# A decoder layer on one Trainium2 core: five edits to the order of background work and to the weight buffers

## The chip, the cores and the metric

The kernel is one launch on one core of a Trainium2 chip. The metric is device time in microseconds (us), the median of repeated runs; less is better. The core has a matmul engine (PE, and PEld for its weight loads), a vector engine (DVE), a scalar engine (ACT), GpSimd (POOL), and SyncE (SP), which issues most of the DMAs.

## The reference

One inference step of one hybrid decoder layer for 512 prompt tokens and 32 sample tokens (8 sequences of 4), model width 2048, all in float32:

```python
xn = rmsnorm(x, g_mix)
q, k, v, iq, ik, iw, xb, yb, qm = split(xn @ w_in)
o_attn = dsa_attend(...)        # indexer scores, top-k keys per query, softmax over those keys
o_lru = rg_lru(conv4(xb)) * gelu(yb)
o_mem = softmax(qm @ mk.T * MEM_SCALE) @ mv
gates = sigmoid(xn @ w_gate)
x = x + sum_n(gates[n] * (o[n] @ w_br[n])) @ w_o
h = rmsnorm(x, g_ffn)
s = (h @ w_peer_q) scored against two sets of 128 sub keys per head, 8 heads; top 16 of the 16 x 16 sums
y = sum over the chosen 16384-row experts of  softmax(s) * gelu(u[e] . h) * v[e]
out = rmsnorm(x + y, g_final)
```

The sample tokens read paged key and value caches, and states of the convolution and of the recurrence.

## The kernel before

**Products.** Every float32 weight chunk of 128 x 1024 (512 KB) is streamed once: SP issues the DMA into a tile `raw` (L242), ACT rounds it to `hi` (L222), DVE forms `lo = raw - hi` (L223), and PE multiplies hi by the high and low part of the activations and lo by the high part, so 24 matmuls of up to 320 columns for one chunk in the last stage. `raw` has a ring of RAW = 3 buffers, `hi` and `lo` of HL = 3 (L173); `widen(stack, raw, hl)` (L230) adds buffers from a pool that lives as long as the stack.

**Order of work.** The 544 tokens are done in two parts: columns 0 to HA - 1 and the rest. The program is written as a foreground of projections with four queues of generators beside it (`bg`, `bg2`, `bg3`, `bg4`, class `Background`, L141). `pump()` runs in the foreground's inner loop, and each queue advances by its `rate` for eight pumps. Each engine executes its instructions in the order in which the program issues them, and so does SP's queue of DMAs. The rates therefore fix the order of the instructions on each engine.

**Stages.** Memory keys and norms to about 300 us; `branches(0)` to about 600; `merge` (L922) of the first part to 1060; `output_proj` to 1150; queries of the first route; `branches(1)`, 1300 to 1792; `merge(HA, ...)` to 2206; `output_proj(HA, ...)` to 2338; the second route's queries, each followed by one `up` (L1310), to 2600; gate matrices with further ups to 2914; then 16 groups of eight `z` (L1432) and `down` (L1447), to 4473, and the last norm. In `branches(1)` the indexer's rounds of maximum and replacement run on DVE (L637, L638), attention heads (L820 scores, L830 transposes of the softmax `ex`, L837 values) sit in `bg2`, memory heads (L485 scores, L491 transposes of `mex`) in `bg`, and eight recurrence channels (`lru`, L736) in `bg4`, each entered after its two projections xb and yb. The experts of the first 96 prompt tokens are gathered row by row beside all this (`bg3`): POOL issues a 1 MB gather (L1189), paced by a matmul, and DVE multiplies it (L1237 for u, L1245 for v), some 2.3 us each, in three `row` buffers.

**The last stage.** `ups` 0 to 49 (AHEAD_UP = 50) are done before it, each stored to DRAM (`ge_dram`, L1317) and read back as `gl` (L1428) when its z is formed; from group 6 on the ups run beside the downs. `zh` and `zl` have ZB = 16 buffers, `gl` has GL = 4, and the stage has no added `raw` buffers. `acc` (2.5 MB) is loaded before group 0's down (L1464).

Of the kernel before, what the change touches and what calls it, by code (L numbers as in the profile page):

```python
# [8 lines left out]
F = mybir.dt.float32  # L9
# [3 lines left out]
AF = mybir.ActivationFunctionType  # L13
OP = mybir.AluOpType
# [9 lines left out]
HA = NS + SEQ // 2  # L24
# [14 lines left out]
NX = NG - 128  # L39
NTA = T - NG  # L40
N1 = HA - NG
GL = 4
ZB = 16
AHEAD_UP = 50

CH_Q, CH_K, CH_V, CH_IQ, CH_IK, CH_XB, CH_YB, CH_QM, NCH = 0, 8, 10, 12, 20, 21, 29, 37, 45
# [130 lines left out]
def program(tc, ins, outs):  # L177
    nc = tc.nc
# [212 lines left out]
    def branches(part):  # L391
# [154 lines left out]

        def mem_channels():
            for h in range(4):
                qm = []
                for i in range(2):  # L550
                    s = staged(CH_QM + 2 * h + i)
                    if first:
                        nc.vector.tensor_copy(qms[:, 2 * h + i], s[:, :P0])
                    qm.append(s)
                bg.add(mem_head(h, qm))
# [177 lines left out]
            nc.sync.dma_start(scv, ins["sconv"])  # L733
            nc.sync.dma_start(slr, ins["slru"])

        def lru(c, xb, yb):  # L736
            def v(i):
                return vec[:, i + c:i + c + 1]

# [52 lines left out]
            if first:  # L792
                nc.gpsimd.tensor_copy(hl[:, c, 1:], bt(hs)[:, :, NT - 1])
            yield
            nc.scalar.activation(ig, yb, AF.Gelu_apprx_tanh)
            nc.vector.tensor_tensor(ig, hs, ig, op=OP.mult)
            nc.sync.dma_start(o_dram[8 + c, :, cols], ig)
            yield
# [96 lines left out]
        if first:  # L895
            bg2.add(*[attn_sample(pr) for pr in range(NB // 2)])
        bg4.rate = 2.2
        bg2.rate = 2.2 if first else 1.1
        if not first:
            memo = ExitStack()  # L900
            open_memory()
            bg.rate = 0.8
            mem_channels()
        for c in range(8):
            xb = staged(CH_XB + c)
            yb = staged(CH_YB + c)
            bg4.add(lru(c, xb, yb))
        bg2.drain()
        bg.drain()
        bg4.drain()  # L910
# [11 lines left out]
    def merge(c0, x, mp_, side):  # L922


        mo = ([], [])
        n_ = x[0].shape[-1]
        os_ = ExitStack()
        op_ = pool(f"lm{c0}", os_, side=side)
        m = [mp_.tile([128, n_], F, name=f"m{e}", tag="ml", bufs=ND + 1) for e in range(ND)]
        for i, n in enumerate((2, 0, 1)):  # L930
            op = ([op_.tile([128, n_], R, name=f"oh{k}") for k in range(8)],
                  [op_.tile([128, n_], R, name=f"ol{k}") for k in range(8)])
            with urgent():
                for k in range(8):
                    raw = op_.tile([128, n_], F, name="oraw", tag="sg", bufs=4)
                    nc.sync.dma_start(raw, o_dram[8 * n + k, :, c0:c0 + n_])
                    split(op[0][k], op[1][k], raw)
            sgs = {}
            for d in range(ND + GLAG):
                if d < ND:  # L940
                    pg = project(ins["w_gate"][n * ND + d], [x], ND, ps_p)
                    sgs[d] = op_.tile([128, n_], F, name="sg", tag="sg", bufs=4)
                    with urgent():
                        nc.scalar.activation(sgs[d], pg, AF.Sigmoid)
                if d < GLAG:
                    continue
                e = d - GLAG
                sg = sgs.pop(e)
                pu = project(ins["w_br"][n, e], [op], 8, ps_p)
                with urgent():  # L950
                    if i == 0:
                        nc.vector.tensor_tensor(m[e], pu, sg, op=OP.mult)
                    else:
                        nc.vector.tensor_tensor(sg, pu, sg, op=OP.mult)
                        nc.gpsimd.tensor_tensor(m[e], m[e], sg, op=OP.add)
                    if i == 2:
                        mo[0].append(mp_.tile([128, n_], R, name=f"mh{e}"))
                        mo[1].append(mp_.tile([128, n_], R, name=f"ml{e}", tag="ml", bufs=ND + 1))
                        split(mo[0][e], mo[1][e], m[e])
        os_.close()  # L960
        return mo

    def output_proj(c0, mo, xg, o0, rs):

        n_ = rs.shape[-1]
        wo = ExitStack()
        wp = pool(f"wp{c0}", wo)
        ssum = wp.tile([128, n_], F, name="ssum")
        for d in range(ND):
            xr = wp.tile([128, n_], F, name="xr", bufs=2)  # L970
            nc.sync.dma_start(xr, ins["xT"][d, :, c0:c0 + n_])
# [4 lines left out]
            nc.sync.dma_start(x2_dram[d, :, c0:c0 + n_], x2)  # L976
            scaled_split(xg[0][:, d, o0:o0 + n_], xg[1][:, d, o0:o0 + n_], x2, V_GFFN + d)
            add_square(ssum, x2, wp.tile([128, n_], F, name="sq"), d == 0, nc.vector if d >= 12 else nc.gpsimd)
        inv_rms(rs, ssum, n_, ps_w, "w1")
        wo.close()  # L980


    branches(0)
# [9 lines left out]
    xgfs = ExitStack()  # L993
    xgfp = pool("xgf", xgfs, side="right")
    xgF = [xgfp.tile([128, ND, HA], R, name=f"xgF{i}") for i in range(2)]
    output_proj(0, mF, xgF, 0, rs[:, :HA])
    mfs.close()

    gs_ = ExitStack()
# [294 lines left out]
    for d in range(ND):  # L1294
        x2 = map_.tile([128, N1], F, name="x2r", bufs=2)
        nc.sync.dma_start(x2, x2_dram[d, :, NG:HA])
        scaled_split(xgd[0][:, d, :N1], xgd[1][:, d, :N1], x2, V_GFFN + d)
    output_proj(HA, mA, xgd, N1, rs[:, HA:])
    wide.close()
    mas.close()  # L1300
    rps = ExitStack()
# [79 lines left out]
                yield  # L1381
            nc.sync.dma_start(g_dram[g0 + i], gs)

    for t, (c0, rows) in enumerate(tiles):
        token_rms(3 + t, HA + c0, rows)
    xg2 = [x[:, :, N1:] for x in xgd]
    bg.rate = 1.2
    bg3.rate = 0.3
    share["pool"] = 0
    pairs(route2, lambda c: query(c, xg2, HA), up)  # L1390
    ups = iter(range(16, AHEAD_UP))
    while bg.queue:
        up(next(ups))
# [10 lines left out]
    bg2.rate = 2.8  # L1404
    bg3.rate = 0.85
    for j in ups:
        up(j)
    bg2.drain()
    ras.close()
    rts.close()  # L1410
# [5 lines left out]
    zp = pool("zp", zs0)  # L1416
    acc = zp.tile([128, ND, NTA], F, name="acc")
    zt = {}

    def gated(j):  # L1420
        if j % 4 == 0:
# [35 lines left out]
    for g in range(16):  # L1457
        bg3.rate = 0.52 if 8 * g < AHEAD_UP else 0.72
        for j in range(8 * g + 2 if g else 0, min(8 * g + 10, 128)):
            if j >= AHEAD_UP:  # L1460
                up(j)
            gated(j)
        if g == 0:
            nc.sync.dma_start(acc, x2_dram[:, :, NG:].rearrange("k p t -> p k t"))  # L1464
        down(g)
    inv_rms(ssum, ssum, NTA, ps_w, "w1")
# [53 lines left out]
```

## Time and profile before

| | us |
|---|---|
| median of 3 runs | 4498.55 (4497.03 to 4500.84) |
| the profiled execution | 4492.66 |
| its span in the trace | 4490.9 |
| PE busy | 4179.3 (93%) |
| DVE busy | 3440.3 (77%) |
| ACT busy | 1931.0 (43%) |
| POOL busy | 1164.4 (26%) |
| DMA moved | 1232.82 MB, 275 GB/s over the span |

Busy time is a mean over stages. An engine that waits is shown with the releaser that ended the wait, in the form [idle <-releaser]. A row of the timeline gives start and length in us, engine, line, operation and tiles; SPq rows are DMA issues. PEclk and the granted clock are shares of full speed, and 0.5 is the lower of the two levels (1.2 of 2.4 GHz).

### The profile page before, as it was taken

The page shows a single profiled execution, that of the slowest core. Times are in us where ns is not written, and L with a number is a line of the kernel's source. Part 1 is how long each engine was busy: PE and PEld are TensorE (multiplying, and loading weights), DVE is VectorE, ACT ScalarE, POOL GpSimd, SP SyncE. Part 2 cuts the span into 40 slices and gives each one's busy share as a digit, 9 for nine tenths or more (in the row PEclk, how much of TensorE's full clock was granted, in tenths as well). Part 3 has the DMA queues.
Part 4 walks back from the last instruction along what each step waited for, and adds up shares of the span by engine and source line. Part 5 has one row for each costly group of instructions (what it writes and reads, how often), then busy time and mean ns, then how long its engine had stood idle before and what let it go on. Part 6 is the DMA issues. An engine that isn't in the chain of part 4 may idle for free. (4 is left out here: it accounts for less than half of the span.)

```text
span 4490.9 us, 75736 instructions
## 1 busy us (share of the span) xinstructions
PE 4179.3 (93%) x29283; PEld 3985.9 (89%) x29283; DVE 3440.3 (77%) x5235; ACT 1931.0 (43%) x2942; POOL 1164.4 (26%) x1295
## 2 busy tenths in 40 slices
PE   8999899999989776999889899989999999999998
PEld 7869699999977765999889899989999999999897
DVE  6547444455788876898888899979877899887887
ACT  5434653344433348444443368633333333333333
POOL 3022410001244233244333331212122222222223
PEclk9999999999999988999999999989999999999999
DMA  7656555556545766999996679999969999997995
GB/s 261 227 191 219 156 161 176 165 175 196 177 141 181 264 231 218 354 385 370 345 330 234 235 272 360 372 355 357 329 230 348 357 360 361 359 345 270 351 367 194
DMA packets 383562, 1232.82 MB, mean 275 GB/s; under 512 B 51552, under 2 KB 169056, under 8 KB 322272
## 3 DMA queue, kind: packets, MB, share of 16 engines
q1 hardware_dynamic: 314592, 747.69, 49.2%
q0 software_dynamic: 68608, 480.28, 27.9%
q8 instruction: 230, 3.77, 0.3%
q14 instruction: 132, 1.08, 0.1%
HBM read 1167.50 MB, written 60.22 MB: 273 GB/s over the span
## 5 line engine op out<-in xcount | busy, mean ns | idle before, releaser
L222 ACT CAST hi<-raw 128x1024 fp32r<-128x1024 f32 x1140 | 1191.6, 1049 | 1661.2 <-PE mm L272 661.0
L223 DVE TENSOR_TENSOR lo<-raw,hi 128x1024 fp32r<-128x1024 f32 x1140 | 1425.6, 1254 | 532.7 <-ACT hi L222 526.0
L272 PE MATMUL mm<-xgd,hi 128*128 128x320 f32 (+1 forms) x4608 | 1025.2, 311 | 8.0 <-ACT hi L222 8.0
L272 PEld LDWEIGHTS mm<-xgd,hi 128*128 128x128 f32 x4608 | 776.0, 191 | 9.7 <-ACT hi L222 9.5
L272 PE MATMUL mm<-xgd,lo 128*128 128x320 f32 (+1 forms) x2304 | 720.3, 313 | 28.8 <-DVE lo L223 28.5
L1447 PE MATMUL mm<-zh,hi 128*128 128x320 f32 x2048 | 636.0, 311 | 39.3 <-ACT zh L222 24.3
L1447 PE MATMUL mm<-zh,lo 128*128 128x320 f32 x2048 | 638.9, 312 | 9.7 <-DVE lo L223 9.6
L1447 PE MATMUL mm<-zl,hi 128*128 128x320 f32 x2048 | 634.9, 310 | 0.0
L272 PE MATMUL mm<-xF,hi 128*128 128x288 f32 x2976 | 618.2, 301 | 0.6 <-DVE xF L223 0.6
L272 PE MATMUL mm<-xA,hi 128*128 128x256 f32 x2976 | 556.9, 288 | 19.7 <-ACT hi L222 19.6
L1189 POOL DMA_INDIRECT row<-in_un,idx x224 | 323.5, 1444 | 934.5 <-PE mm L272 224.3
L1245 DVE SCALAR_TENSOR_TENSOR gacc<-row,hv,gacc 128x2048 f32<-128x2048 f32 x221 | 523.0, 2367 | 28.6 <-DMA row<-in_vn,idx 14.1
L1189 POOL DMA_INDIRECT row<-in_vn,idx x224 | 325.4, 1453 | 844.4 <-PE mm L272 209.3
L1237 DVE SCALAR_TENSOR_TENSOR row<-row,xnat 128x2048 f32<-128x2048 f32 x224 | 515.1, 2299 | 21.7 <-DMA row<-in_un,idx 12.3
L272 PEld LDWEIGHTS mm<-xA,hi 128*128 128x128 f32 x2976 | 469.4, 193 | 47.8 <-issue 25.8
L272 PEld LDWEIGHTS mm<-xF,hi 128*128 128x128 f32 x2976 | 481.9, 188 | 22.3 <-issue 18.8
L272 PEld LDWEIGHTS mm<-xgd,lo 128*128 128x128 f32 x2304 | 439.9, 191 | 39.7 <-DVE lo L223 39.1
L272 PE MATMUL mm<-xF,lo 128*128 128x288 f32 x1488 | 445.7, 300 | 0.0
L272 PE MATMUL mm<-xA,lo 128*128 128x256 f32 x1488 | 429.4, 289 | 12.8 <-DVE lo L223 12.6
L1447 PEld LDWEIGHTS mm<-zh,hi 128*128 128x128 f32 x2048 | 386.8, 189 | 41.9 <-ACT zh L222 24.8
L1447 PEld LDWEIGHTS mm<-zh,lo 128*128 128x128 f32 x2048 | 386.7, 189 | 18.5 <-DVE lo L223 18.1
L1447 PEld LDWEIGHTS mm<-zl,hi 128*128 128x128 f32 x2048 | 386.7, 189 | 0.6 <-DVE zl L223 0.5
(374 smaller groups left out, 6349.8 us busy)
## 6 DMA issues: line engine op xcount, KB each, us to landing
raw<-in_u SPq DMA_DIRECT2D x256, 512.0 KB, 7.1
raw<-in_v SPq DMA_DIRECT2D x256, 512.0 KB, 6.8
raw<-in_w_gate SPq DMA_DIRECT2D x192, 512.0 KB, 5.2
raw<-in_w_in SPq DMA_DIRECT2D x180, 512.0 KB, 4.6
raw<-in_w_br SPq DMA_DIRECT2D x96, 512.0 KB, 4.1
raw<-in_w_o SPq DMA_DIRECT2D x64, 512.0 KB, 4.8
raw<-in_w_pq SPq DMA_DIRECT2D x64, 512.0 KB, 4.2
g_dram<-gs SPq DMA_DIRECT2D x10, 2048.0 KB, 10.4
```

The source lines that it names most:

```text
L222: nc.scalar.copy(hi, src)
L223: eng.tensor_tensor(lo, src, hi.bitcast(F), op=OP.subtract)
L272: last["mm"] = nc.tensor.matmul(p[:, i, :n], a[:, s], chunk(b[which], u + k), start=(u + k == 0 and pr == 0), stop=(u + k == k_chunks - 1 ...
L1189: i = nc.gpsimd.indirect_dma_start(out=r, out_offset=None, in_=ins[table], in_offset=bass.IndirectOffsetOnAxis(ap=ind[:, s:s + 1], axis=0))
L1237: j = nc.vector.scalar_tensor_tensor(r, r, 1.0, xn, op0=OP.mult, op1=OP.mult, accum_out=h)
L1245: j = nc.vector.scalar_tensor_tensor(acc, r, h, acc, op0=OP.mult, op1=OP.add)
L1447: last["mm"] = nc.tensor.matmul(p[:, 0, :NTA], a[:, s], b, start=(k == 0 and pr == 0), stop=(k == 7 and pr == 2))
```

## The change

1. In `branches(1)` the attention queue `bg2` stands still (rate 0.0 in place of 1.1) until memory head 2 is entered, then runs at 1.15; `bg` runs at 1.0 in place of 0.8. In both parts each `lru` is entered after its first projection xb, and waits with its gelu until yb is there.
2. In the last branch of the second `merge`, the adds of e >= 8 go to DVE in place of POOL.
3. `output_proj` returns its `inv_rms` as a closure; in the second part this runs after the projection of query 0 (with `ssum` in a longer-lived pool), and `token_rms` after query 2.
4. The last three of the 50 early ups are issued after the first ten z, ahead of group 0's down.
5. The last stage gets two more `raw` buffers (`widen(zs0, 2, 0)`); ZB falls from 16 to 13 and GL from 4 to 3.

```diff
-GL = 4
-ZB = 16
+GL = 3
+ZB = 13
...
         def mem_channels():
             for h in range(4):
+                if h == 2 and not first:
+                    bg2.rate = 1.15
...
-        def lru(c, xb, yb):
+        def lru(c, xb, late):
...
-            nc.scalar.activation(ig, yb, AF.Gelu_apprx_tanh)
+            while not late:
+                yield
+            nc.scalar.activation(ig, late[0], AF.Gelu_apprx_tanh)
...
-        bg2.rate = 2.2 if first else 1.1
+        bg2.rate = 2.2 if first else 0.0
...
-            bg.rate = 0.8
+            bg.rate = 1.0
...
-            xb = staged(CH_XB + c)
-            yb = staged(CH_YB + c)
-            bg4.add(lru(c, xb, yb))
+            late = []
+            bg4.add(lru(c, staged(CH_XB + c), late))
+            late.append(staged(CH_YB + c))
...
-                        nc.gpsimd.tensor_tensor(m[e], m[e], sg, op=OP.add)
+                        adds = nc.vector if c0 and i == 2 and e >= 8 else nc.gpsimd
+                        adds.tensor_tensor(m[e], m[e], sg, op=OP.add)
...
-        ssum = wp.tile([128, n_], F, name="ssum")
+        ssum = (sums or wp).tile([128, n_], F, name="ssum")
...
-        inv_rms(rs, ssum, n_, ps_w, "w1")
         wo.close()
+        return lambda: inv_rms(rs, ssum, n_, ps_w, "w1")
...
-    output_proj(HA, mA, xgd, N1, rs[:, HA:])
+    finish = output_proj(HA, mA, xgd, N1, rs[:, HA:], xgp)
...
-    for t, (c0, rows) in enumerate(tiles):
-        token_rms(3 + t, HA + c0, rows)
...
-    pairs(route2, lambda c: query(c, xg2, HA), up)
+
+    def between(c):
+        if c == 0:
+            finish()
+        if c == 2:
+            for t, (c0, rows) in enumerate(tiles):
+                token_rms(3 + t, HA + c0, rows)
+        up(c)
+
+    pairs(route2, lambda c: query(c, xg2, HA), between)
...
     for j in ups:
-        up(j)
+        if j < AHEAD_UP - 3:
+            up(j)
...
+    widen(zs0, 2, 0)
...
         if g == 0:
+            for j in range(AHEAD_UP - 3, AHEAD_UP):
+                up(j)
             nc.sync.dma_start(acc, x2_dram[:, :, NG:].rearrange("k p t -> p k t"))
```

**Place 1: PE in the second part, where attention head 0 waits for the last rounds of selection.** Before (mm is a projection, ex the attention's softmax, kT the keys):

```order
L272 MATMUL mm_16981<-xA1_87,hi_17035 128x256
L272 MATMUL mm_16981<-xA0_86,lo_17036 128x256
L830 MATMUL w1_16221<-cst_75,ex_16189 128x128 x3
L820 MATMUL w1_16260<-kT_91,qh_16178 128x512
L830 MATMUL w1_16301<-cst_75,ex_16266 128x128 x4
L837 MATMUL w1_16328<-pT_16182,vN_92 128x256 x3
```

Now, the first attention scores on PE in this part (they carry L824; mex is the memory heads' softmax):

```order
L272 MATMUL mm_17187<-xA0_86,lo_17232 128x256
L491 MATMUL w1_16387<-cst_75,mex_16382 128x128 x2
L497 MATMUL w1_16428<-mpT_16330,mv_16327 128x256 x2
L497 MATMUL w1_16464<-mpT_16330,mv_16327 128x256 x2
L824 MATMUL w1_16500<-kT_91,qh_16495 128x384
L485 MATMUL w1_16528<-mk_16523,stage_16300 128x256
L485 MATMUL w1_16528<-mk_16523,stage_16402 128x256
L491 MATMUL w1_16539<-cst_75,mex_16534 128x128 x2
L834 MATMUL w1_16558<-cst_75,ex_16506 128x128 x3
```

Memory head 0 now stands where attention head 0 stood: its scores (L485) come at place 9199 of PE's order, its transposes (L491) at 9519 and 9618, and the attention's first scores at 9621; before, these were at 9095 and its first transposes at 9517.

**Place 2: PE behind the last projection of the second part.** Before:

```order
L272 MATMUL mm_18774<-xA0_86,lo_18778 128x256
L764 MATMUL w1_18282<-xc_18263,w_rg_18280 128x256
L764 MATMUL w1_18303<-xc_18263,w_ig_18301 128x256
L764 MATMUL w1_18449<-xc_18430,w_rg_18447 128x256
L764 MATMUL w1_18470<-xc_18430,w_ig_18468 128x256
L764 MATMUL w1_18599<-xc_18592,w_rg_18597 128x256
L764 MATMUL w1_18605<-xc_18592,w_ig_18603 128x256
```

Now (L766 is the recurrence's gate product, L764 before):

```order
L272 MATMUL mm_18774<-xA0_86,lo_18778 128x256
L834 MATMUL w1_17990<-cst_75,ex_17946 128x128 x3
L824 MATMUL w1_18047<-kT_91,qh_17706 128x512
L834 MATMUL w1_18082<-cst_75,ex_18053 128x128 x4
L841 MATMUL w1_18115<-pT_17939,vN_92 128x256 x3
L841 MATMUL w1_18115<-pT_17939,vN_92 128x128
L824 MATMUL w1_18166<-kT_91,qh_17937 128x384
L766 MATMUL w1_18182<-xc_18151,w_rg_18180 128x256
L766 MATMUL w1_18203<-xc_18151,w_ig_18201 128x256
L834 MATMUL w1_18216<-cst_75,ex_18172 128x128 x3
L824 MATMUL w1_18271<-kT_91,qh_17937 128x512
L834 MATMUL w1_18312<-cst_75,ex_18277 128x128 x4
```

Behind the last projection three recurrence channels remain, as before, and now one and a half attention heads as well.

**Place 3: SP's queue at the start of the last stage.** Before:

```order
L242 DMA raw_31895<-in_v 128x1024
L1423 DMA gt_31648<-g_dram_85 128x10x128
L1317 DMA ge_dram_82<-ge_31637 128x320
L1428 DMA gl_31652<-ge_dram_82 128x320
L1428 DMA gl_31659<-ge_dram_82 128x320
L1428 DMA gl_31666<-ge_dram_82 128x320
L1428 DMA gl_31673<-ge_dram_82 128x320
```

Now (L1323 is the store of an up's result, L1443 its load, L1438 the gate's load):

```order
L242 DMA raw_31586<-in_u 128x1024
L1323 DMA ge_dram_82<-ge_31356 128x320
L1438 DMA gt_31441<-g_dram_85 128x10x128
L1443 DMA gl_31445<-ge_dram_82 128x320
L1443 DMA gl_31452<-ge_dram_82 128x320
L1443 DMA gl_31459<-ge_dram_82 128x320
L242 DMA raw_31723<-in_v 128x1024
L1323 DMA ge_dram_82<-ge_31427 128x320
```

Before, the first `gl` stood behind the store of the last up; now they stand ahead of the stores of the last ups, and the first `raw` of a down behind three of them.

## Rows read from the trace of the kernel before

**Rows 1.** The page: span, and busy time by engine.

```profile
span 4490.9 us, 75736 instructions
PE 4179.3 (93%) x29283; PEld 3985.9 (89%) x29283; DVE 3440.3 (77%) x5235; ACT 1931.0 (43%) x2942; POOL 1164.4 (26%) x1295
```

**Rows 2.** Windows: length, busy time of each engine, clock, DMA share, GB/s.

```profile
1552.00:1600.00 48.00, 7.77 (x25) 5.25 (x25) 38.59 (x55) 7.45 (x11) 15.82 (x10) 0.54 0.67 243
1750.00:1800.00 50.00, 7.73 (x26) 4.91 (x24) 19.69 (x51) 37.24 (x49) 7.22 (x13) 0.55 0.32 103
1850.00:2200.00 350.00, 348.94 (x2943) 348.31 (x2942) 316.60 (x291) 156.62 (x201) 150.09 (x93) 1.00 0.98 379
2650.00:2900.00 250.00, 247.01 (x1798) 244.67 (x1797) 236.74 (x364) 198.39 (x459) 55.02 (x40) 0.99 0.94 360
2956.00:3300.00 344.00, 340.80 (x2291) 339.08 (x2292) 297.18 (x351) 118.17 (x143) 77.19 (x50) 0.99 0.94 341
3300.00:4400.00 1100.00, 1067.09 (x7131) 1050.34 (x7130) 933.56 (x1028) 384.10 (x492) 260.45 (x220) 0.99 0.91 336
```

**Rows 3.** Timeline of PE, parts one and two: rows that end an idle time.

```profile
554.19 1.92 PE L859 MATMUL w<-kp,qs 128*32 128x512 f32 x4 [8.21 <-DMA kp<-in_ck,idx]
...
1567.06 0.90 PE L830 MATMUL w<-cst,ex 128*128 128x128 f32 x3 [12.93 <-DVE ex L457]
1596.30 1.08 PE L830 MATMUL w<-cst,ex 128*128 128x128 f32 x4 [26.63 <-DVE ex L457]
...
1801.04 0.80 PE L272 MATMUL mm<-xA,hi 128*128 128x256 f32 x2 [18.28 <-ACT hi L222]
```

**Rows 4.** Timeline of DVE, second part, inside the last rounds of selection.

```profile
1571.97 2.35 DVE L1245 SCALAR_TENSOR_TENSOR gacc<-row,hv,gacc 128x2048 f32<-128x2048 f32 x1 [2.45 <-DMA row<-in_vn,idx]
```

**Rows 5.** Timeline of ACT, end of part two: two recurrence channels, last step.

```profile
1771.25 0.42 ACT L795 ACTIVATE g<-stage 128x256 f32<-128x256 f32 x1
...
1781.58 0.42 ACT L795 ACTIVATE g<-stage 128x256 f32<-128x256 f32 x1
```

**Rows 6.** Timeline of DVE, then POOL, then PE, end of the second merge.

```profile
2211.78 2.81 DVE L1245 SCALAR_TENSOR_TENSOR gacc<-row,hv,gacc 128x2048 f32<-128x2048 f32 x1
...
2210.90 1.54 POOL L955 TENSOR_TENSOR m<-m,sg 128x256 f32<-128x256 f32 x1
2215.06 0.77 POOL L955 TENSOR_TENSOR m<-m,sg 128x256 f32<-128x256 f32 x1 [2.62 <-DVE sg L954]
...
2221.68 0.58 PE L272 MATMUL mm<-mh,hi 128*128 128x256 f32 x1 [15.18 <-ACT hi L222]
```

**Rows 7.** Timeline of ACT, then PE, around the second inv_rms.

```profile
2335.42 1.04 ACT L222 CAST hi<-raw 128x1024 fp32r<-128x1024 f32 x1 [7.77 <-DMA raw<-in_u]
...
2338.51 1.22 PE L286 MATMUL w<-ssum,ones 128*128 128x256 f32 x2 [10.00 <-DVE ssum L303]
...
2346.26 1.33 PE L272 MATMUL mm<-xgd,hi 128*128 128x320 f32 x4 [2.64 <-ACT hi L222]
```

**Rows 8.** Timeline of SP, then PE, at the start of the last stage.

```profile
2926.49 2.18 SPq L1317 DMA_DIRECT2D ge_dram<-ge  x1
...
2935.55 0.64 PE L1447 MATMUL mm<-zh,hi 128*128 128x320 f32 x1 [21.11 <-ACT zh L222]
```

**Rows 9.** Groups of instructions, 2956 to 4473 us: busy, mean ns, idle before.

```profile
L1447 PE MATMUL mm<-zh,lo 128*128 128x320 f32 x2016 | 628.3, 312 | 9.0 <-DVE lo L223 8.9
L1447 PE MATMUL mm<-zh,hi 128*128 128x320 f32 x2016 | 625.5, 310 | 18.2 <-ACT hi L222 12.1 <-ACT zh L222 3.2 <-DVE acc L1450 2.9
...
L272 PE MATMUL mm<-xgd,hi 128*128 128x320 f32 x2496 | 555.9, 311 | 5.3 <-ACT hi L222 5.3
L223 DVE TENSOR_TENSOR lo<-raw,hi 128x1024 fp32r<-128x1024 f32 x406 | 495.0, 1220 | 150.1 <-ACT hi L222 149.3
...
L1245 DVE SCALAR_TENSOR_TENSOR gacc<-row,hv,gacc 128x2048 f32<-128x2048 f32 x126 | 295.9, 2348 | 3.1 <-PE mm L1447 2.3 <-PE mm L272 0.4 <-DMA row<-in_vn,idx 0.3
L1237 DVE SCALAR_TENSOR_TENSOR row<-row,xnat 128x2048 f32<-128x2048 f32 x116 | 264.9, 2283 | 11.1 <-DMA xnat<-xn_dram 5.7 <-DMA row<-in_un,idx 4.3 <-PE mm L272 0.9
```

More of the change, by code (lines that the diff above doesn't have):

```diff
@@ L961, in merge, with output_proj @@
         return mo
-    def output_proj(c0, mo, xg, o0, rs):
+    def output_proj(c0, mo, xg, o0, rs, sums=None):
         n_ = rs.shape[-1]
@@ L995, in program @@
     xgF = [xgfp.tile([128, ND, HA], R, name=f"xgF{i}") for i in range(2)]
-    output_proj(0, mF, xgF, 0, rs[:, :HA])
+    output_proj(0, mF, xgF, 0, rs[:, :HA])()
     mfs.close()
```

## The prediction

> **What bounds the kernel now.** I read the page first: PE is busy for 4179.3 of 4490.9 us [rows 1], so what can be won is the rest, some 312 us, and the question for each edit is which idle time of PE it touches. The table of windows comes next, because it shows where PE stands still and what the other engines and the DMAs do there [rows 2]. Then the timeline gives the single waits, each with its releaser [rows 3 to 8], and the groups of the last stage give the many small ones [rows 9].
>
> The reader is to see three kinds of stretch. At 1552 to 1600 and at 1750 to 1800 PE works 7.77 and 7.73 us, at a mean clock of 0.54 and 0.55: DVE is in the first the engine that is late, ACT in the second. At 1850 to 2200 and 2650 to 2900 PE loses 1.1 of 350 and 3.0 of 250 us. In the last stage it loses 3.2 of 344 and then 32.9 of 1100 us, although DMA share (0.91) and DVE (933.56 of 1100) are lower there than in the two good stretches [rows 2]. So the last stage isn't short of bandwidth or of DVE time as a whole; it is short of depth: DVE's lo waits 149.3 us for ACT's hi, and PE's waits end with hi or lo [rows 9].
>
> **The change part by part.** Gains are positive; all are against the profiled execution (4492.66 us; its span, 4490.9, leaves 1.8 us outside). It lies 5.9 us under the median of the runs, 4498.55, and I take the same savings from the median.
>
> *Recurrence begun earlier, first part.* PE waits 8.21 us for a page of keys [rows 3]. In the new order 51 more matmuls stand on PE between the first and the second sample's scores (2729 places from the stage's order before, 2780 now). At 0.1186 us (348.94 us over 2943 matmuls of 256 columns [rows 2]; these have 288) that covers about 6 us. It could be nothing, if the pages move by as much, and 8.2 at most. I take 6.
>
> *Second part, the waits on DVE.* PE waits 12.93 and 26.63 us, 39.6 together, for the attention's softmax, which stands on DVE among the selection's rounds and the expert rows [rows 3]; one such row product takes 2.35 us and there waited 2.45 us for its DMA [rows 4]. The change puts memory head 0 in the attention's place. But its softmax stands among the same rounds on DVE: in the order five full row products come between its first maximum and its second result, eight between the corresponding ones of the attention before. What is new is that 96 projection matmuls stand between the two waits, 96 x 0.1186 = 11.4 us of cover, while 103 fewer (318 for 421) stand ahead of the first, 12.2 us less. DVE sets this stretch, so the two nearly cancel, and what is left is the three row products that the softmax no longer waits for, 3 x 2.35 = 7.0, less three lo of 1.22 [rows 9] that now lie between: 3.4. I take 4; the ends are 11.4, if all of the cover counts, and -3, if one row more lands as late as the one shown.
>
> *Second part, the tail.* The three recurrence channels left behind the last projection run at ACT's pace, 1781.58 - 1771.25 = 10.33 us each [rows 5], and PE resumes at 1801.04 [rows 3]. Three are left now too, since the gelu still waits for yb, and one and a half attention heads with them. Nothing is lost if the heads fit into ACT's free time; at most, a head costs what a channel does, 15.5. I take a loss of 7, about the middle: the window shows ACT busy for 37.24 of 50 us, so some room is there, but a quarter only [rows 2].
>
> *Adds on DVE, second merge.* PE waits 15.18 us at the end of this merge [rows 6]. The chain is multiplication on DVE, add on POOL (0.77 us, from 2215.06), then the loads of w_o that take over the released buffer. Now DVE makes the add itself, but in its order an expert row's product (2.35) stands between the two, where before it stood ahead of the multiplication; three further adds queue ahead. From the gacc's start at 2211.78: 0.4 for the multiplication, 2.35, 0.4 for the add, 1.2 for the three adds make 2216.1, against 2215.83 before. I take 0, ends -1.5 and 1.5. The rows show more: this gacc took 2.81 us beside a POOL add that took 1.54, against 2.35 [rows 9] and 0.77 alone. The Trainium skill's "SBUF — State Buffer" (Who interferes with whom) says that a DVE instruction with two SBUF inputs contends with a GpSimd instruction that reads SBUF. The trace agrees by these two pairs; by the rule the eight adds that leave POOL would give back up to 8 x 0.46 = 3.7 us of DVE time and the sum would be some 3 us better if DVE bound this merge.
>
> *inv_rms behind query 0.* The 10.00 us wait goes from PE's order, but ACT stood 7.77 us before 2335.42 for a weight chunk, and the last activations' split comes behind it on ACT and DVE; the query's last eighth needs that split too. Then PE stops anyway until the first up's chunk has been rounded, at 2346.26 after 2.64 us [rows 7]. Before, 35 of the query's 48 matmuls ran ahead of the wait. I take 1; ends 0 and 4.
>
> *Three ups beside the first z.* PE stands 21.11 us, because the store of the last up (issued at 2926.49) and the reload follow each other on SP's queue [rows 8]; then 2.9 us for acc [rows 9]. In the new order the loads are issued ahead of the last stores, and three ups of 48 matmuls are PE's work meanwhile: 144 x 0.150 (1067.09 over 7131 [rows 2]) = 21.5 us. DVE in the same time has, from the first z product to z7's low part, 16 small operations of 0.48, six lo of 1.22, five row products of 2.3 and three up results of 0.48: 28 us. PE gets to z7 only 3.2 us after the ups. So 3 to 4 us stay open, with perhaps 4 more where z4 to z7 wait for their loads behind the v chunks. Of 24.0 I take 16, ends 8 and 24. If ups were not there to cover it, all 21 us would stay.
>
> *Two raw buffers more in the last stage, three z and one gl less.* The loss there is 36.1 us of idle PE [rows 2]. At the rate of the merge with five raw buffers (1.1 of 350) 4.5 us of it would stay, at that of the ups with four (3.0 of 250) 17. The savings are 31 and 19; I take 25. From nothing (were the rows or the hi ring the limit) to 36 is possible. ZB = 13 lets three more z be formed before the present down ends (ten are live), where 16 let six. That matters at the five boundaries without ups between the downs, where PE lost 3.2 us in all [rows 2]. The first late z is needed five z, 15 x 0.150 = 2.3 us, after the boundary, and takes three steps of 0.48: I count nothing; up to 4 us each if its load is late too.
>
> Sum: 6 + 4 - 7 + 0 + 1 + 16 + 25 = 45, and 4498.55 - 45 = 4453.5, say **4453 us**. 0.2% (9 us) is about what a measurement of this kernel can tell from no change.
>
> **The rivals.**
> *A: the raw buffers give nothing.* For it: DMA share is 0.91 to 0.94 [rows 2], and a chunk that is loaded earlier still waits for ACT, DVE and three hi buffers. Against it: the merge drew 379 GB/s where this stage draws 336. Time: 4453 + 25 = 4478.
> *B: the second part loses.* The waits on DVE stay at 39.6 and the tail grows by 15.5, as the rounds set the one and the channels the other: 4 + 8.5 worse, 4466.
> *C: too few z buffers.* Five groups lose 4 us each: 4473. Against it: PE loses least there now, 3.2 of 344 us [rows 2], so the z are early.
> *D: slower, by the expert rows.* There are 242 row products in the last stage [rows 9], 6.3 us apart; their 1 MB gathers go through POOL's queue beside SP's chunks, and DVE executes in order, so a late row holds up the lo behind it. DVE has 166 us free in the 1100 [rows 2], or 0.95 us for each of some 175 rows there (242 x 1100 / 1517). Now only 4.6 us are lost to late rows [rows 9]. If two more chunks in flight make each row 1.2 us later, DVE is full and 0.25 x 175 = 44 us come on top, with no gain from the buffers: 4478 + 44 = 4522. It decides from 0.95 us of lateness on. The Trainium skill's "DMA: Bandwidth & Descriptors" (Issuing engines are not separate DMA queues) says that DMAs issued by different engines run on the same 16 DMA engines and interleave. No run here yet shows whether it costs the rows anything; the sum by it would be D's.
> *E: better.* The last stage falls to the merge's rate, the waits on DVE shrink by 11 and z begins without a stop: 6 + 7 + 8 more, 4432.
>
> **How the numbers follow.** Forecast 0.45, A 0.18, B 0.12, C 0.10, D 0.05, E 0.10. The range runs from E's time less what rms and tail could add (4 and 7), 4420, to A with a few us of B, 4484, and leaves out D, and combinations of A, B and C. Faster by over 0.2% means below 4489.5: all but D and the worst combinations, 0.89; within 0.2%: A with B or C, 0.06; slower: D, 0.05.
>
> **What would show it.** Last stage right: PE's idle time in 3300 to 4400 (shifted) falls from 33 to about 10, and hi is no longer released by the DMA of raw for most of ACT's waits. z begin right: in place of the 21.11 us one or more waits of 3 to 8 us in all. Second part right: two or three waits on mex and ex of about 35 us in all, and a stop before the merge that is longer by about 7. Rms: the 10 us wait moves to the first up or to the query's last eighth and stays. The prediction is wrong if DVE's waits for rows in the last stage grow from 4.6 us to over 100, if PE waits for zh there, or if the second part ends later than before by over 10 us.

## The result

The changed kernel takes 4446.9 us (median of 4 runs, 4443.24 to 4452.73) where before takes 4497.79 in the same comparison; the ratio is 0.9888, with a 95% interval of 0.9871 to 0.9905, so 43 to 58 us faster. The forecast was 4453, between 4420 and 4484. The profiled execution took 4444.03 us, its span is 4442.3.

The page of the changed kernel, to be held against [rows 1]:

```profile
span 4442.3 us, 75719 instructions
PE 4168.0 (94%) x29283; PEld 3990.3 (90%) x29283; DVE 3442.7 (77%) x5243; ACT 1931.7 (43%) x2941; POOL 1210.8 (27%) x1287
```

PE's busy time fell by 11.3 us, so 37.3 of the 48.6 us of span are idle time that went. Where it went is read by cutting both traces at the same instructions. The cuts are the first matmul of the first merge's branch products, of the first w_o product, of the second part's indexer, of the second merge's branch products, of the second w_o product, and then the last accumulation of groups 0, 5 and 15 of the last stage:

| stretch | before | changed | |
|---|---|---|---|
| start to first merge's branch products | 617.3 | 619.1 | +1.8 |
| first merge, to w_o | 441.6 | 445.3 | +3.7 |
| w_o, first route, to the second part | 249.3 | 248.8 | -0.5 |
| second part | 498.8 | 489.8 | -9.0 |
| second merge | 414.6 | 411.5 | -3.1 |
| second w_o to the end of group 0 | 782.8 | 783.6 | +0.8 |
| groups 1 to 5 | 283.6 | 280.9 | -2.7 |
| groups 6 to 15 | 1183.9 | 1144.0 | -39.9 |

The sum is -48.9, and 0.3 us are lost behind the last cut. Each kernel was traced in one execution. The last stage gives most, the second part some, and the stretch around the first z nothing.

**The last stage.** Windows of the changed kernel; the columns are those of [rows 2]:

```profile
2960.00:3300.00 340.00, 339.93 (x2313) 339.04 (x2313) 297.02 (x347) 118.14 (x143) 85.16 (x50) 1.00 0.94 345
3300.00:4340.00 1040.00, 1030.83 (x7013) 1027.76 (x7012) 921.50 (x1014) 380.48 (x485) 314.10 (x217) 1.00 0.94 350
```

PE now loses 9.2 us of 1040 where it lost 32.9 of 1100. The groups of the same stage show why (busy, mean ns, idle before), to be held against [rows 9]:

```profile
L223 DVE TENSOR_TENSOR lo<-raw,hi 128x1024 fp32r<-128x1024 f32 x409 | 498.8, 1220 | 27.4 <-ACT hi L222 26.5
L222 ACT CAST hi<-raw 128x1024 fp32r<-128x1024 f32 x409 | 429.5, 1051 | 714.3 <-PE mm L1462 484.5 <-PE mm L272 177.3 <-issue 36.3
...
L1251 DVE SCALAR_TENSOR_TENSOR gacc<-row,hv,gacc 128x2048 f32<-128x2048 f32 x126 | 297.3, 2359 | 24.9 <-DMA row<-in_vn,idx 16.5 <-PE mm L272 4.4 <-PE mm L1462 3.5
L1243 DVE SCALAR_TENSOR_TENSOR row<-row,xnat 128x2048 f32<-128x2048 f32 x118 | 269.9, 2287 | 35.1 <-DMA row<-in_un,idx 14.5 <-DMA xnat<-xn_dram 11.6 <-PE mm L1462 4.2
```

The row of ACT's hi in the kernel before, same view:

```profile
L222 ACT CAST hi<-raw 128x1024 fp32r<-128x1024 f32 x406 | 426.6, 1051 | 822.6 <-DMA raw<-in_v 318.4 <-DMA raw<-in_u 220.5 <-PE mm L1447 176.0
```

ACT stood 539 us for a chunk's DMA; now it stands for PE to release a hi buffer, so the chunk is there before it is wanted. DVE's wait for hi fell from 149.3 to 26.5 us. What rival D spoke of is there, too: waits for expert rows went from 4.6 to 31.0 us (16.5 + 14.5), but DVE has the time for it.

**The second part and the other waits.** PE's timeline in the changed kernel, rows that end an idle time, and the last projection before the tail; against [rows 3], [rows 6] and [rows 7]:

```profile
567.55 1.05 PE L863 MATMUL w<-kp,qs 128*32 128x512 f32 x4 [1.78 <-DMA kp<-in_ck,idx]
581.75 1.09 PE L872 MATMUL w<-cst,ex 128*128 128x128 f32 x4 [4.52 <-DVE ex L457]
598.15 0.53 PE L272 MATMUL mm<-xF,hi 128*128 128x288 f32 x2 [2.13 <-ACT stage L426]
...
1577.53 0.69 PE L491 MATMUL w<-cst,mex 128*128 128x128 f32 x2 [22.90 <-DVE mex L457]
1607.67 0.69 PE L491 MATMUL w<-cst,mex 128*128 128x128 f32 x2 [6.10 <-DVE mex L457]
...
1738.34 0.28 PE L272 MATMUL mm<-xA,lo 128*128 128x256 f32 x1
1746.17 1.08 PE L834 MATMUL w<-cst,ex 128*128 128x128 f32 x4 [4.45 <-DVE ex L457]
1762.21 1.08 PE L834 MATMUL w<-cst,ex 128*128 128x128 f32 x4 [5.09 <-DVE ex L457]
1796.88 0.79 PE L272 MATMUL mm<-xA,hi 128*128 128x256 f32 x2 [18.90 <-ACT hi L222]
...
2214.50 0.58 PE L272 MATMUL mm<-mh,hi 128*128 128x256 f32 x1 [12.98 <-ACT hi L222]
...
2329.92 0.58 PE L272 MATMUL mm<-xgd,hi 128*128 128x256 f32 x1 [7.98 <-ACT xgd L295]
2339.30 1.33 PE L272 MATMUL mm<-xgd,hi 128*128 128x320 f32 x4 [4.93 <-ACT hi L222]
```

The two waits of 12.93 and 26.63 us are now 22.90 and 6.10. Behind the last projection PE needs 58.3 us until it resumes (1738.62 to 1796.88); before it was 49.4, from the row

```profile
1751.32 0.28 PE L272 MATMUL mm<-xA,lo 128*128 128x256 f32 x1
```

to 1801.04. The wait for inv_rms became one for the activations' last split and a longer one for the up's chunk.

**The first z.** SP, then DVE, then PE in the changed kernel, against [rows 8]:

```profile
2913.14 10.99 SPq L242 DMA_DIRECT2D raw<-in_v  x4
2924.18 0.43 SPq L1443 DMA_DIRECT2D gl<-ge_dram  x1
...
2938.33 0.49 DVE L1447 TENSOR_TENSOR gl<-gl,gt 128x320 f32<-128x320 f32 x1 [10.81 <-DMA gl<-ge_dram]
...
2895.06 0.90 PE L272 MATMUL mm<-xgd,hi 128*128 128x320 f32 x2 [4.94 <-ACT hi L222]
2913.16 0.41 PE L272 MATMUL mm<-xgd,lo 128*128 128x320 f32 x1 [2.30 <-DVE lo L223]
2939.36 1.17 PE L1462 MATMUL mm<-zh,hi 128*128 128x320 f32 x3 [12.04 <-ACT zh L222]
```

The wait of 21.11 us is gone, and three others, 19.3 us in all, stand in its place. The longest is for the fifth z: its load goes out at 2924.18, behind the v chunks, and DVE can use it at 2938.33.

### The profile page after: what moved, and what is told of

The parts are those of the page before. It is cut to its first block, busy times and chain, and to the rows that moved or that the text cites. A ratio compares the mean times of both kernels' runs of the same rounds, so it can differ in the third digit from the quotient of the medians.

```text
span 4442.3 us, 75719 instructions
## 1 busy us (share of the span) xinstructions
PE 4168.0 (94%) x29283; PEld 3990.3 (90%) x29283; DVE 3442.7 (77%) x5243; ACT 1931.7 (43%) x2941; POOL 1210.8 (27%) x1287
## 4 chain that ended last, share of the span: by engine, by line
PE 47%; DVE 9%; DMA 4%; issue 3%; ACT 1%; POOL 1%; DVEq 0%; SPq 0%; ACTq 0%; POOLq 0%
PE mm L272 25%; PE mm L1462 19%; DVE lo L223 3%; PE w L1360 2%; DVE gacc L1251 2%; DVE row L1243 1%; DMA row<-in_vn,idx 1%; DMA x2r<-x_dram 1%; DMA gl<-ge_dram 1%; DMA row<-in_un,idx 1%; POOL cand L1103 0%; DMA raw<-in_u 0%; DMA xnat<-xn_dram 0%; DMA raw<-in_w_in 0%; ACT hi L222 0%
## 5 line engine op out<-in xcount | busy, mean ns | idle before, releaser
L1195 POOL DMA_INDIRECT row<-in_un,idx x224 | 354.8, 1584 | 902.1 <-PE mm L272 274.3
L1195 POOL DMA_INDIRECT row<-in_vn,idx x224 | 358.5, 1600 | 789.4 <-PE mm L272 266.5
```

Source lines behind the costliest of these rows:

```text
L1195: i = nc.gpsimd.indirect_dma_start(out=r, out_offset=None, in_=ins[table], in_offset=bass.IndirectOffsetOnAxis(ap=ind[:, s:s + 1], axis=0))
```

## The experiments

Kernels of one set ran on one chip, each set beside before on that chip. Chips differ in the first part by more than the edits do (617 to 657 us up to the first merge), so the stretches behind it are compared over all sets, and the first part only within one. The stretches of a row are those of one traced execution, and of before there is only the trace of the table above. From the same cuts:

| kernel | ratio to before, interval | second part | w_o 2 to end of group 0 | groups 1 to 5 | groups 6 to 15 |
|---|---|---|---|---|---|
| e1_raw_alone | 0.9928 (0.9900 to 0.9955) | 500.2 | 790.1 | 287.0 | 1131.0 |
| e2_no_raw | 0.9965 (0.9951 to 0.9979) | 488.7 | 781.1 | 278.2 | 1198.6 |
| e3_ups_back | 0.9870 (0.9847 to 0.9892) | 490.6 | 791.6 | 281.5 | 1131.6 |
| e7_z_small | 1.0024 (1.0005 to 1.0044) | 498.6 | 783.4 | 288.4 | 1190.2 |
| e4_late_lru | 1.0049 (1.0032 to 1.0066) | 505.3 | 787.8 | 280.1 | 1186.3 |
| e5_rates | 0.9991 (0.9977 to 1.0006) | 493.6 | 783.7 | 284.5 | 1180.7 |
| x_gl5 | 0.9871 (0.9854 to 0.9889) | 491.8 | 776.0 | 281.9 | 1138.0 |
| x_ups5 | 0.9864 (0.9839 to 0.9890) | 488.7 | 775.3 | 291.1 | 1136.7 |
| x_raw4 | 0.9899 (0.9865 to 0.9932) | 494.0 | 777.3 | 283.4 | 1147.3 |
| x_ups5_gl5 | 0.9865 (0.9837 to 0.9894) | 496.0 | 774.8 | 289.3 | 1138.9 |
| e9_lru_first_old | 0.9885 (0.9852 to 0.9917) | 491.9 | 785.2 | 281.1 | 1142.8 |
| x_best | 0.9867 (0.9842 to 0.9891) | 494.5 | 776.9 | 286.3 | 1131.4 |

**The buffers alone.** My theory after the result was that the last stage lacked loaded chunks; the rival was that the moved ups set another phase.

```diff
-GL = 4
-ZB = 16
+GL = 3
+ZB = 13
...
     zt = {}
+    widen(zs0, 2, 0)
```

> The kernel before with edit 5 alone (two more raw buffers, ZB 13, GL 3). Theory (the last stage lacked depth of loaded chunks): from the end of group 0's down to the end of the last the trace of the change is 43 us shorter, and nothing else touches that stretch, so this kernel should be 38 to 48 us faster than before (about 4455 where before is 4498), and DVE's wait of lo for hi in the stage should fall from 149 to under 40 us. Rival (the gain there comes mostly from the three ups that were moved, which leave SP's queue and the row gathers at another phase): under 20 us faster.

Faster by 20 to 45 us, 32 in the middle: my 38 is inside the interval, the rival's 20 at its end, and the trace decides. Groups 6 to 15 are as short as in the change, and hi and lo behave as there (groups of the last stage):

```profile
L223 DVE TENSOR_TENSOR lo<-raw,hi 128x1024 fp32r<-128x1024 f32 x409 | 497.6, 1217 | 29.4 <-ACT hi L222 28.6
L222 ACT CAST hi<-raw 128x1024 fp32r<-128x1024 f32 x409 | 429.1, 1051 | 698.0 <-PE mm L1448 463.5 <-PE mm L272 183.4 <-issue 24.3
```

What is missing was lost at the stage's start: 790.1 against 782.8, and PE waited 24.68 us for the first z where it had waited 21.11.

**The change without the buffers.**

```diff
-GL = 3
-ZB = 13
+GL = 4
+ZB = 16
...
     zt = {}
-    widen(zs0, 2, 0)
```

> The change without edit 5 (no added raw buffers, ZB 16, GL 4), all else as changed. Theory of depth: the 43 us are lost again, about 4490, and what is left of the change is 5 to 9 us of gain over before. Rival (the parts interact, so that the rest is worth more without the buffers): under 4480.

16 us faster than before (9 to 22), more than the 5 to 9 that I expected. There is no sign of an interaction in the sum, within intervals as wide as these: 32 + 16 = 48, and the change has 50. The last stage is back to its old state, by the row

```profile
L223 DVE TENSOR_TENSOR lo<-raw,hi 128x1024 fp32r<-128x1024 f32 x405 | 494.0, 1220 | 149.5 <-ACT hi L222 147.5
```

The start of the stage shows what the held ups do without edit 5. PE no longer stands for the first z, but it stands for the ups' own weight chunks:

```profile
2901.95 0.63 PE L272 MATMUL mm<-xgd,lo 128*128 128x320 f32 x1 [5.83 <-DVE lo L223]
2926.80 0.90 PE L272 MATMUL mm<-xgd,hi 128*128 128x320 f32 x2 [12.28 <-ACT hi L222]
...
2898.04 8.93 SPq L1480 DMA_DIRECT2D acc<-x_dram  x1
2907.07 8.20 SPq L242 DMA_DIRECT2D raw<-in_u  x2
```

The chunk of the longer wait was issued behind the 2.5 MB of `acc`, and ACT began to round it at 2925.71. The stretch up to group 0's end takes 781.1 us, against 782.8 to 787.8 in the three kernels with the old ups and the old rings (before, e4, e5).

**The price of the smaller z rings.** Before, with ZB 13 and GL 3 only:

```diff
-GL = 4
-ZB = 16
+GL = 3
+ZB = 13
```

> The kernel before with ZB 13 and GL 3 but no more raw buffers: the price of edit 5 alone. Theory: nothing at five of the six boundaries, 0 to 5 us slower in all, since the z are early there. Rival (prediction's case C): some 20 us slower, with PE waiting for zh at the ends of groups 0 to 4, and then the buffers are worth 60, not 43.

11 us slower (2 to 20): the theory's 0 to 5 and the rival's 20 both lie at the interval's ends. In the stretches it shows 4.8 us in groups 1 to 5, 0.6 up to group 0's end and 6.3 in groups 6 to 15, where the five kernels with three raw buffers scatter by 18. So there is a price, but the interval reaches from almost nothing to the rival's 20, and where it arises stays open: the rival's mechanism isn't there, as no wait of PE in groups 1 to 5 ends with zh. The buffers without their price are the distance of this kernel from e1, some 43 us of the whole time.

**One buffer in place of two.**

```diff
-    widen(zs0, 2, 0)
+    widen(zs0, 1, 0)
```

> The change with one added raw buffer in the last stage in place of two. Between the ends of groups 5 and 15 the kernels with three raw buffers took 1180.7 to 1198.6 us, those with five 1131.0 to 1144.0. Theory of depth: four buffers give most of it, 1140 to 1160, as the first added chunk takes up the usual wait and the second only the rare long ones. Rival (the gain has a threshold at five, or comes from how the pool lies): 1175 or more.

Groups 6 to 15 take 1147.3 us. With three buffers the five kernels average 1187.9 (1183.9, 1198.6, 1190.2, 1186.3, 1180.7), with five the eight average 1136.8 (1131.0 to 1144.0): the first added buffer gives about 41 us, the second about 10. This is the theory of depth, with no threshold at five. That the second gives anything rests on one execution, 3 us outside the range of the eight.

**The ups back in their place.**

```diff
     for j in ups:
-        if j < AHEAD_UP - 3:
-            up(j)
+        up(j)
...
-            for j in range(AHEAD_UP - 3, AHEAD_UP):
-                up(j)
```

> The change with edit 4 undone: all 50 early ups ahead of the first z. The trace of the change shows the end of group 0's down 6.4 us earlier than before, where the stage ahead stood 6.7 us earlier already, so the theory says that the three moved ups gave nothing: the time is within 4 us of the change (4443 to 4451), and the wait of 21 us before the first z is back. Rival, which is my prediction's own term: 16 us slower, about 4463. A second rival: without them the loads of z and the first v chunks no longer collide, and it is 3 to 8 us faster than the change.

58 us under before on its chip (49 to 69), the change 50 on its own (43 to 58): no loss, so the whole time rules out that the move gave 16; a few us it can't tell. The stretches say more. Up to group 0's end it takes 791.6 us against 783.6, and PE stands longer at the first z:

```profile
2942.53 0.63 PE L1461 MATMUL mm<-zh,hi 128*128 128x320 f32 x1 [24.16 <-ACT zh L222]
2953.57 0.41 PE L1461 MATMUL mm<-zh,hi 128*128 128x320 f32 x1 [4.50 <-ACT zh L222]
```

So beside edit 5 the held ups do win some 8 us there, and edit 5 with the old ups loses about 7 (782.8 to 790.1). In the change the two cancel. They don't add up, though: without edit 5 the held ups won only 1.7 (782.8 to 781.1), which the scatter of 5 between kernels with the same code there doesn't set apart from nothing, and with the held ups edit 5 loses 2.5. Groups 6 to 15 were 12 us shorter here than in the change, which is more than the ups should touch; kernels with the same code in that stretch differ by as much, so nothing follows from it.

**GL 5, ZB 12.**

```diff
-GL = 3
-ZB = 13
+GL = 5
+ZB = 12
```

> The change with GL 5 and ZB 12 in place of 3 and 13 (the same memory). In the change PE stands 12.04 us at the first z, because the load of the fifth z stands on SP's queue behind seven v chunks and lands 14 us after its issue. Theory (the gl ring puts it there): with five buffers the first five loads go ahead of the v chunks and that wait falls to under 8 us; 2 to 8 us faster than the change in the stretch from the gate matrices' end to group 0's end (223.5 us in the change). Rival (ZB decides): one z buffer less makes the boundaries of groups 0 to 4 longer by over 1 us each, and nothing is won.

776.0 against 783.6: 7.6 us, as the theory of the ring says. The longest wait at the first z is now

```profile
2970.24 0.63 PE L1462 MATMUL mm<-zl,hi 128*128 128x320 f32 x1 [4.95 <-DVE zl L223]
```

and groups 1 to 5 aren't longer (281.9). The ratio, 0.9871, can't be told from the change's.

**Five ups held back.**

```diff
-        if j < AHEAD_UP - 3:
+        if j < AHEAD_UP - 5:
...
-            for j in range(AHEAD_UP - 3, AHEAD_UP):
+            for j in range(AHEAD_UP - 5, AHEAD_UP):
```

> The change with five ups held back beside the first z in place of three. Theory: the two further ups are 96 matmuls, 14 us of work for PE while the z are loaded; if the loads keep their place, the waits at the start of the stage (4.94 + 2.30 + 1.59 + 12.04 in the change) fall by 6 to 12 us and the time is 5 to 10 us below the change. Rival: the chunks of the two ups only stand in front of the z loads on SP's queue, the waits move with them, and the time is the same within 3 us.

775.3, or 8.3 us less, but groups 1 to 5 take 291.1, 10 more than in the change. The ratio, 0.9864, can't be told from the change's.

**Both.** The two edits above together.

> The change with five ups held back and GL 5, ZB 12. Each alone shortened the stretch from the second merge's output to group 0's end from 783.6 us to 775.3 and 776.0. Theory (two causes: work for PE, and the fifth load's place on SP's queue): together 768 to 773. Rival (one cause, the same wait): 774 to 777, no better than either.

774.8: no better than either alone, the rival's value; the two remove the same wait. Groups 1 to 5 are long again (289.3), as in the other kernel with five held ups.

**The recurrence alone.** Before, with only the second projection taken late:

```diff
...
-            xb = staged(CH_XB + c)
-            yb = staged(CH_YB + c)
-            bg4.add(lru(c, xb, yb))
+            late = []
+            bg4.add(lru(c, staged(CH_XB + c), late))
+            late.append(staged(CH_YB + c))
```

> The kernel before with the recurrence begun after its first projection, in both parts, and nothing else. From the runs so far the second part (from its first indexer product to the second merge's first branch product) takes 498.6 to 500.2 us with the old order and 488.7 to 490.6 with edit 1. Theory: this half brings nothing, because the gelu waits for yb as before and three channels stay behind the last projection: second part 497 to 501 us, first part (to its merge) within 4 us of 617 to 624, time within 4 us of before. Rival: the channels come earlier and shorten the tail, second part under 494.

22 us slower (14 to 30). Neither theory holds: by the trace it costs in both parts, 505.3 us for the second and 654.7 for the first, against 645.7 in the kernel of the same set that has the old order there. For the first part that is one execution against one, and two other kernels of the set with this same order took 646.9 and 656.6.

**The rates alone.**

```diff
+                if h == 2 and not first:
+                    bg2.rate = 1.15
...
-        bg2.rate = 2.2 if first else 1.1
+        bg2.rate = 2.2 if first else 0.0
...
-            bg.rate = 0.8
+            bg.rate = 1.0
```

> The kernel before with the rates of the second part alone (attention queue still until memory head 2, then 1.15; memory queue 1.0). Theory: all of the 9 to 10 us come from here, because the waits on DVE's softmax fall from 39.6 to about 29 to 30 us (22.90 + 6.10 in the change) and the tail does not grow by the 7 us that I put down: second part 488 to 491 us, 8 to 11 us faster. Rival: the attention heads left over make the tail 5 to 7 us longer without the early recurrence beside it, and the second part takes 493 us or more.

The waits are the change's, as the theory had it:

```profile
1606.46 0.69 PE L491 MATMUL w<-cst,mex 128*128 128x128 f32 x2 [24.59 <-DVE mex L457]
1635.45 0.69 PE L491 MATMUL w<-cst,mex 128*128 128x128 f32 x2 [6.10 <-DVE mex L457]
```

but the whole is only 4 us faster (10 faster to 3 slower), and the second part takes 493.6 us, which is the rival's number, about 6 us under the old order's 498.6 to 500.2. Over the kernels with both halves of edit 1 it is 488.7 to 496.0, 491.8 in the mean of nine. So the early recurrence, which costs 6 alone, costs nothing that can be seen beside the new rates; the 2 us between 493.6 and 491.8 lie inside the scatter of 7.

**The early recurrence in the second part only.** On the change, and on the kernel with five ups and GL 5:

```diff
             late = []
+            if first:
+                xb = staged(CH_XB + c)
+                late.append(staged(CH_YB + c))
+                bg4.add(lru(c, xb, late))
+                continue
```

> The change with the recurrence begun early in the second part only. Theory: in the first part the early start removed the 8.21 us wait for a page, but put waits on the softmax and on the staged projections in its place, so it gains nothing: time within 4 us of the change, first part as long as in the kernels of this chip with the early start. Rival, which is my prediction's term: 4 to 8 us slower than the change.

Its ratio is 0.9885 (0.9852 to 0.9917), the change's value; the interval is too wide to exclude the rival's 4 to 8 us. The trace fits neither: the wait for the page is back, 8.82 us, and still the first part is shorter than in the two kernels of this set with the early start, 637.4 us against 646.0 and 652.7.

> The same, with the recurrence begun early in the second part only. If the early start gains nothing in the first part, the time is that of the kernel with five ups and GL 5 within 4 us, some 8 to 14 us under the change, and the best so far; if it gains there, 4 to 8 us worse.

Its first part takes 634.6, so on this chip the early start costs 9 to 18 us there. In the whole time (4464.68 against 4467.3 for its twin, intervals wide) that can't be told, and with 0.9867 it isn't shown to beat the change. No version did.

## Why the prediction was right, and where it wasn't

The time lay 6 us from the forecast, and that is luck, as misses of opposite sign cancelled: the ups gave 16 us less than forecast and the buffers 18 more, the first part 8 less and the second 12 more. The forecast's main step, that depth of loaded chunks is what the last stage lacks, did hold. Point by point, in the order of the prediction, gains positive:

*Recurrence, first part: 6 predicted, -1.8 found.* The step that failed is that cover for one wait is a gain. The 8.21 us for the page did go (1.78 is left), but 4.52 us for a softmax and 2.13 for a staged projection came in its place. Each set has both orders: old 617.7 and 620.3, early 617.4 and 623.8 in the first; old 645.7, early 654.7, 656.6 and 646.9 in the second; old 637.4 and 634.6, early 646.0 and 652.7 in the third. So the early start wins nothing on one chip and loses 1 to 18 us on the others. In the traces of these two chips PE is idle for 52.1 to 54.4 us of the first part with the old order and for 55.9 to 66.3 with the early start, so part of the loss is more waiting; why was not tried.

*Second part: 4 - 7 predicted, 9 found.* The tail is 8.9 us longer, against 7 predicted. The waits on the selection's rounds fell from 39.6 to 29.0, so by 10.6, the upper end of my range. What I left out is that attention work that is now in the tail was taken from the stretch ahead of it. From the second part's first cut to the last projection it is 425.4 us (1313.2 to 1738.6) where it was 443.4, 18 less. PE's idle time there fell by 6.3 us (65.7 to 59.4): the two waits by 10.6, while smaller ones grew by 4.3. Its busy time fell by 11.7, of which the attention's matmuls are 10.3 (116 where there were 152). That work I charged in the tail without taking it off ahead of it.

*Adds on DVE: 0 predicted, 3 found*, with a wait of 12.98 for 15.18. Nine kernels with the edit average 414.1 us over this merge, five without 416.2; the scatter is 411.2 to 418.2. A term of 2, just above my end of 1.5. The case for it that I had put beside the sum, less contention between DVE and POOL, was not tried by itself.

*inv_rms: 1 predicted, none found.* Waits of 10.00 and 2.64 became 7.98 and 4.93, as the rows on ACT's wait for the chunk had said.

*Three ups beside the first z: 16 predicted, none found in the sum.* The step that failed is the cover: I counted the three ups as 21.5 us of ready work for PE, and left out that their own chunks come over the queue on which acc and the v chunks stand. Without edit 5 (e2) the 24.0 us of waits became 5.83 and 12.28 us for these chunks, and the stretch is 1.7 us shorter than before. With edit 5 another size was wrong: I put 4 us for z4 to z7 behind the v chunks, it was 12.04, and its load stood behind seven v chunks, of which edit 5 lets two more be in flight (with one buffer less the stretch takes 777.3). I costed the two edits one by one; they meet on SP's queue. Beside edit 5 the ups give 6 to 8 us (783.6 and 785.2 against 790.1 and 791.6), and edit 5 with the old ups takes some 7. That PE waits for zh in the last stage was one of my signs of being wrong, and it came, here at the stage's start.

*Buffers: 25 predicted, 42.6 found in groups 1 to 15* (2.7 + 39.9). The step was right in kind, as the experiments show, and even in size for what it counted: PE's idle time in these groups fell from 39.0 to 13.2 us, by 25.8. It was too small because I let only idle time count (36.1). The other 16.8 us are booked as busy: in 3300 to 4400 before, PE's matmuls took 0.1496 us each (1067.09 over 7131), now 0.1470 (1030.83 over 7013). PE's timeline before, around the longest stop of groups 1 to 15, shows two ways in which a stop costs busy time:

```profile
4195.18 0.31 PE L1447 MATMUL mm<-zl,hi 128*128 128x320 f32 x1
4195.33 0.31 PE L1447 MATMUL mm<-zh,lo 128*128 128x320 f32 x1
4201.78 0.63 PE L1447 MATMUL mm<-zh,hi 128*128 128x320 f32 x1 [6.15 <-ACT hi L222]
4202.22 0.47 PE L1447 MATMUL mm<-zl,hi 128*128 128x320 f32 x1
...
4205.34 0.47 PE L1447 MATMUL mm<-zl,hi 128*128 128x320 f32 x1
4205.61 0.46 PE L1447 MATMUL mm<-zh,lo 128*128 128x320 f32 x1
...
4206.05 0.31 PE L1447 MATMUL mm<-zl,hi 128*128 128x320 f32 x1
4206.20 0.31 PE L1447 MATMUL mm<-zh,lo 128*128 128x320 f32 x1
```

and its window of 10 us, where the granted clock is 0.70:

```profile
4200.00:4210.00 10.00, 7.86 (x40) 7.46 (x41) 8.23 (x8) 4.46 (x5) 1.58 (x1) 0.70 0.38 125
```

The first way is the overlap. A matmul is booked for 0.31 us, but the next one starts 0.15 behind it; the last one ahead of a stop has none behind it, so 0.16 us of the stop are booked as busy. Groups 6 to 15 had 50 stops, now 13; this gives about 6 us. The second is the clock. Behind this stop the matmuls start 0.27 us apart up to 4205.9 and 0.15 after that, so it cost about 2 us more. The granted clock was at its lower level for 20.5 us of groups 6 to 15 before and for 10.2 now, which is worth 5 us at most. The rest, some 6, was not followed; matmuls that start late by less than the overlap, with no idle time booked, would be such a loss. The smaller z rings cost something, as e7 shows, where I had counted nothing.

*The rivals.* A didn't happen: the buffers carry most of the gain. D's mechanism is in the rows (waits for expert rows of 4.6 us before, 5.5 in e7, 31.6 in e1 and 31.0 in the change, so they come with the raw buffers) and far from the 166 us at which it would decide. C's price is about half there by the middle of e7's interval, but its mechanism, waits for zh at the ends of groups 0 to 4, is in neither e7's trace nor the change's. B is out: the waits on DVE shrank. Of E, the waits on DVE shrank by 10.6 us as it said; a start of z without a stop didn't come.

## What to carry to other kernels

When an engine's many short waits end with a load, one more buffer ahead of the first step can be worth more than the idle time says, because each stop also costs busy time around it; here the first added buffer gave about 41 us and the second about 10, where 39 were idle. Edits that meet on one in-order queue must be costed together: what is loaded earlier stands ahead of something else. Work that is to cover a wait needs its own loads in time. Work that moves behind a stage's end has to be charged there and taken off ahead of it.

## What the runs showed that I had not expected

The first merge's stretch takes either 441.6 or 445.3 us, and nothing between, in all fourteen profiled executions. It is 441.6 in before, e1, e4, x_gl5, x_ups5, x_raw4 and e9, 445.3 in the change, e2, e3, e5, e7, x_ups5_gl5 and x_best. No edit touches this stretch, and the split follows none (e7 differs from before by two ring sizes of the last stage). PE is busy all the time and the clock is full in both; windows of before and of the change, 700 to 1000 us:

```profile
700.00:1000.00 300.00, 300.00 (x2253) 300.00 (x2252) 145.65 (x149) 117.04 (x149) 19.30 (x24) 1.00 0.56 173
```

```profile
700.00:1000.00 300.00, 300.00 (x2233) 300.00 (x2232) 144.32 (x147) 115.80 (x148) 18.52 (x23) 1.00 0.56 171
```

The 300 us hold 2253 matmuls in the one and 2233 in the other. In the last stage matmuls that follow each other without a stop start 0.1467 us apart in all fourteen traces, so the slower pace belongs to this stretch. 3.7 us of the change's time are this pace, and nothing in its edits explains them. As each kernel has one trace, it isn't known whether a kernel keeps its pace from run to run; what sets it is open.
